# Joining two half-width products into one 512-column product, with the halves added on ScalarE and GpSimd

## The chip, the core and the metric

The kernel runs on one core of a Trainium2 chip. A core has five engines with queues of their own: TensorE (matrix products; "PE" in the profile, its weight loads "PEld"), VectorE ("DVE"), ScalarE ("ACT"), GpSimd ("POOL") and SyncE ("SP", which here only issues transfers). SBUF is the on-chip memory with 128 partitions; PSUM holds the results of products in banks of 128x512 float32. The metric is the device time of one execution in microseconds (us); lower is better.

## The reference

The program is a decoder trunk of two layers over a sequence of 512 positions with 1024 features, in float32. Each layer is a feed-forward block, a mixer (a causal convolution module beside differential attention), and a second feed-forward block:

```python
def swiglu(h, w_gate, w_up, w_down):
    return (jax.nn.silu(h @ w_gate) * (h @ w_up)) @ w_down

for l in range(DEPTH):
    x = x + 0.5 * swiglu(rms_norm(x, ffn1_norm[l]), ffn1_w_gate[l], ffn1_w_up[l], ffn1_w_down[l])
    h = rms_norm(x, mix_norm[l])
    a, g, q, k, v = jnp.split(h @ w_in[l], splits, axis=-1)
    ...
    x = x + jnp.concatenate([conv_out, diff_out], axis=-1) @ w_out[l]
    x = x + 0.5 * swiglu(rms_norm(x, ffn2_norm[l]), ffn2_w_gate[l], ffn2_w_up[l], ffn2_w_down[l])
```

The hidden width `D_FF` is 2816, that is 22 blocks of 128. The change touches the four feed-forward blocks only.

## The kernel before, in words

**Split operands.** Every float32 operand of a large product is held as two parts: a high part in a rounded type (`float32r`) and a low part, the rest. A product is then three products: high weight by high feature, high by low, low by high. The weights come from memory as `wraw` (128x512) and are split in `parts_of` (L101, L102): ScalarE copies into `whi`, VectorE subtracts `raw - hi` into `wlo`. Both operands of that subtraction lie in SBUF. In the mixer some of these subtractions are given to GpSimd instead.

**Seven products.** The 22 hidden blocks of a feed-forward block are done in three parts (`PARTS`): six in the plain way, and two times eight by a scheme in the manner of Strassen and Winograd, which makes two output blocks by two column halves (`HS` = 256 columns each) with seven half-size products instead of eight. For that, sums of weights are formed: `Sums` loads a base with SyncE (`wsum`, L162), adds a second block to it with an accumulating transfer of GpSimd's queue (L160), and two more sums are made on VectorE (L175, L176). Sums of features (`th`, `tl` for the inputs; `yh`, `yl` for the hidden values) are made on VectorE.

- `seven` does the gate and up projections of one hidden block, called a group below. It has 16 groups in a feed-forward block, 64 in the program. Its products are named by weight and feature: `u2u1`/`t1`, `u2`/`t4`, `g1`/`b11`, `g2`/`b21`, `all`/`b22`, `g1u2u1`/`t2`, and in `rest` `g1u1`/`t3`. Each is a loop over four contraction blocks with three products of 256 columns, L434. It uses two PSUM banks; `a`, `d` are the halves of the first and `b`, `c` of the second. ScalarE copies partial results into the SBUF tile `keep` (L439, L443, L448), VectorE combines them (L451, L456, L457, L460), and ScalarE applies the silu (L452).
- `rest` of a group is run as `before()` within the next group, between its second and third products (t4 and b11).
- `Hidden.add` makes the hidden values' parts (L483, L484) and their sums (L489 to L494).
- `Pair` does the same seven products for two output blocks of the down projection: `head`, `body` and `finish`, with products at L523. There are four pairs after each part of eight, 32 in the program; the first of each four (`m == 0`) has an order of its own, and the very last one ends in `finish_halves`.

**What sets the order.** A scheduler of the framework orders each engine's instructions from dependences and its own estimate; the first product of each loop is kept in program order (`keep_in_program_order`), and some splits are held behind named instructions (`behind`). Buffers are rings: 9 `whi`, 9 `wlo`, 5 `wraw`, 4 `wsum`, three pairs of PSUM banks, 2 `keep`. Each engine does its queue strictly in that order, so an instruction that waits holds those behind it.

Of the kernel before, what the change touches and what calls it, by code (L numbers as in the profile page):

```python
# [18 lines left out]
P = 128  # L19
# [51 lines left out]
def trunk(ctx: ExitStack, tc: tile.TileContext, xt, par, lamv, relb, onehot,  # L71
# [12 lines left out]
    def f32(ap):  # L84
        return ap.bitcast(F32)
# [120 lines left out]

    x = act.tile([P, KT, SEQ], F32, tag="x", name="x")

    acth = act.tile([P, KT, SEQ], F32R, tag="acth", name="acth")
    actl = act.tile([P, KT, SEQ], F32R, tag="actl", name="actl")  # L210
# [11 lines left out]
    S.activation(small.tile([P, 1], F32, tag="first", name="first", bufs=1), f32(ones_r[:, P : P + 1]), AF.Copy)  # L222
# [152 lines left out]
    class Halves:  # L375
# [4 lines left out]
        def __init__(self, fp, pr, r):  # L380
            self.th = fp.tile([P, 3, KT // 2, HS], F32R, tag="th", name="th")
            self.tl = fp.tile([P, 3, KT // 2, HS], F32R, tag="tl", name="tl")

            self.whole = []
            four = [fp.tile([P, 4, SEQ], F32, tag=tag, name="hn") for tag in ("yh", "yl")]
            free = [t[:, n] for t in four for n in range(4)]
# [27 lines left out]

    saves = []

    def seven(halves, w, banks, fp, before, last):
# [7 lines left out]
        g = keep[:, 0::2]  # L425
# [12 lines left out]
        go(c, "u2u1", "t1", first=True)  # L438
        S.activation(keep[:, 3], c, AF.Copy)  # L439
        go(d, "u2", "t4", first=True)  # L440
        before()
        go(a, "g1", "b11")
        S.activation(keep[:, :2], banks[0].rearrange("p (n c) -> p n c", n=2), AF.Copy)  # L443
        go(b, "g2", "b21")
        if not last:
            go(c, "all", "b22")
        go(a, "g1u2u1", "t2")
        saves.append(S.activation(keep[:, 2], a, AF.Copy))  # L448
        if last:
            go(c, "all", "b22")  # L450
# [3 lines left out]
        def rest(out=None):  # L454
            go(a, "g1u1", "t3")
# [9 lines left out]
    class Hidden:  # L465

        def __init__(self, fp, n):
            self.fp, self.n, self.parts = fp, n, [None] * (2 * n)
            self.th = fp.tile([P, 3, n, HS], F32R, tag="yh", name="yh")
            self.tl = fp.tile([P, 3, n, HS], F32R, tag="yl", name="yl")  # L470

        def add(self, mm, rest):
# [8 lines left out]
            hi = self.fp.tile([P, SEQ], F32R, tag=f"hh{mm}", name="hh")  # L481
            lo = self.fp.tile([P, SEQ], F32R, tag=f"hl{mm}", name="hl")
            self.big = S.activation(hi, h, AF.Copy)  # L483
            V.tensor_tensor(lo, h, f32(hi), op=ALU.subtract)  # L484
            self.parts[k] = hi, lo
# [11 lines left out]
        def get(self, name):  # L497
# [4 lines left out]
            return lambda j: tuple(t[:, c : c + HS] for t in self.parts[k0 + j])  # L502

    class Pair:

        def __init__(self, hid, fp, m, m2):
            self.hid, self.m, self.m2 = hid, m, m2
            self.kc, self.kd = (1, 3) if m == 0 else (3, 1)
# [681 lines left out]
```

## Time and profile before

| | |
|---|---|
| median of 3 runs | 1769.01 us (1768.8 to 1769.22) |
| the profiled execution | 1769.0 us, span 1767.2 us |
| TensorE busy | 1758.8 us |
| VectorE busy | 1472.1 us |
| ScalarE busy | 1037.1 us |
| GpSimd busy | 515.7 us |
| granted TensorE clock | 1.000 |

The span is the time from the first to the last instruction. Busy time is the time in which an engine has at least one instruction in work. Products overlap in TensorE's pipeline, so the mean duration of one (283 ns at L434) is longer than the spacing at which they follow each other. A row of the groups reads: line, engine, operation, output and inputs, shapes, count, then busy us and mean ns of one, then the engine's idle time just before them and what ended it. In the timeline a row begins with its start and its duration in us. In the table of stages a row gives, after the stretch and its length, the busy us of each engine and its instructions, then the granted clock, the share of the DMA engines and GB/s.

### The profile page before, as it was taken

What the parts mean: (1) busy time and instruction counts of PE and PEld (TensorE: products, weight loads), DVE (VectorE), ACT (ScalarE), POOL (GpSimd) and SP (SyncE); (2) the same over time, 40 slices, a digit from 0 to 9 for tenths busy, and PEclk for the clock granted to TensorE, in tenths of its full rate; (3) what the DMA queues carried; (4) which work ended last, traced back from release to release, by engine and by line L of the source; (5) the groups of instructions that cost most, each with busy time, mean ns of one, the idle gap of its engine ahead of it and who ended that gap; (6) DMA issues with size and microseconds to landing.
All of it is one profiled execution on the core that took longest, in us unless ns stands there. A gap on an engine that the chain in (4) does not pass through costs nothing.

```text
span 1767.2 us, 32964 instructions
## 1 busy us (share of the span) xinstructions
PE 1758.8 (100%) x11852; PEld 1621.2 (92%) x11852; DVE 1472.1 (83%) x2646; ACT 1037.1 (59%) x1955; POOL 515.7 (29%) x497
## 2 busy tenths in 40 slices
PE   9999999999999999999999999999999999999998
PEld 7799999988788899999988999999887888999998
DVE  7969888969877969989987798999698678698887
ACT  6546566755865436566644565666559554465664
POOL 1011112169970011212200121121798600112122
PEclk9999999999999999999999999999999999999999
DMA  7457777533223457677544576776231234576774
GB/s 229 129 138 185 172 188 190 138 120 100 68 78 114 126 129 178 171 198 179 141 143 111 147 177 172 198 166 166 91 114 49 96 102 139 134 183 163 201 183 127
DMA packets 166613, 257.78 MB, mean 146 GB/s; under 512 B 19271, under 2 KB 63318, under 8 KB 166448
## 3 DMA queue, kind: packets, MB, share of 16 engines
q1 hardware_dynamic: 129600, 201.25, 35.5%
q0 software_dynamic: 36416, 54.12, 18.7%
q8 instruction: 93, 1.52, 0.4%
q14 instruction: 72, 0.59, 0.1%
q10 hardware_dynamic: 432, 0.29, 0.1%
HBM read 253.48 MB, written 3.42 MB: 145 GB/s over the span
## 4 chain that ended last, share of the span: by engine, by line
PE 97%; DVE 1%; POOL 1%; ACT 1%; issue 0%; DVEq 0%; POOLq 0%
PE ps_pair L434 37%; PE ps_pair L523 18%; PE ps_pair L200 9%; PE ps_pair L203 9%; PE ps_pair L204 9%; PE ps_out L200 2%; PE ps_out L203 2%; PE ps_out L204 2%; PE ps_pair L842 2%; PE ps_pair L843 2%; PE ps_pair L841 2%; PE ps_sc L958 1%; PE ps_v L872 1%; PE ps_v L873 1%; PE ps_v L871 1%; POOL wlo L102 0%
## 5 line engine op out<-in xcount | busy, mean ns | idle before, releaser
L101 ACT ACTIVATE whi<-wraw 128x512 fp32r<-128x512 f32 x744 | 452.9, 627 | 397.4 <-PE ps_pair L203 166.3
L102 DVE TENSOR_TENSOR wlo<-wraw,whi 128x512 fp32r<-128x512 f32 x640 | 426.2, 685 | 111.5 <-ACT whi L101 104.2
L160 POOL DMA_DIRECT2D wsum<-in_gu x128 | 112.0, 904 | 700.4 <-DMA wsum<-in_gu 270.7
L434 PE MATMUL ps_pair<-acth,wlo 128*128 128x256 f32 x1024 | 289.8, 283 | 0.0
L434 PE MATMUL ps_pair<-actl,whi 128*128 128x256 f32 x1024 | 289.8, 283 | 0.0
L434 PE MATMUL ps_pair<-acth,whi 128*128 128x256 f32 x1024 | 289.8, 283 | 0.0
L434 PE MATMUL ps_pair<-th,whi 128*128 128x256 f32 x768 | 217.3, 283 | 0.0
L434 PE MATMUL ps_pair<-tl,whi 128*128 128x256 f32 x768 | 217.3, 283 | 0.0
L434 PE MATMUL ps_pair<-th,wlo 128*128 128x256 f32 x768 | 217.3, 283 | 0.0
L200 PE MATMUL ps_pair<-acth,whi 128*128 128x512 f32 x512 | 200.7, 394 | 0.3 <-DVE gs L653 0.3
L203 PE MATMUL ps_pair<-actl,whi 128*128 128x512 f32 x512 | 199.7, 390 | 0.0
L204 PE MATMUL ps_pair<-acth,wlo 128*128 128x512 f32 x512 | 199.3, 390 | 0.0
L434 PEld LDWEIGHTS ps_pair<-actl,whi 128*128 128x128 f32 x1024 | 196.6, 192 | 0.2
L434 PEld LDWEIGHTS ps_pair<-acth,whi 128*128 128x128 f32 x1024 | 196.6, 192 | 0.2
L434 PEld LDWEIGHTS ps_pair<-acth,wlo 128*128 128x128 f32 x1024 | 196.6, 192 | 0.0
L160 POOL DMA_DIRECT2D wsum<-in_dn x112 | 98.9, 1112 | 269.4 <-DMA wsum<-in_dn 55.7
L434 PEld LDWEIGHTS ps_pair<-th,whi 128*128 128x128 f32 x768 | 147.5, 192 | 0.0
L434 PEld LDWEIGHTS ps_pair<-tl,whi 128*128 128x128 f32 x768 | 147.5, 192 | 0.0
L434 PEld LDWEIGHTS ps_pair<-th,wlo 128*128 128x128 f32 x768 | 147.5, 192 | 0.0
L102 POOL TENSOR_TENSOR wlo<-wraw,whi 128x512 fp32r<-128x512 f32 x104 | 137.4, 1345 | 30.4 <-ACT whi L101 19.4
L523 PE MATMUL ps_pair<-hh,whi 128*128 128x256 f32 x512 | 144.9, 283 | 0.0
L523 PE MATMUL ps_pair<-hl,whi 128*128 128x256 f32 x512 | 144.9, 283 | 0.0
(209 smaller groups left out, 4446.5 us busy)
## 6 DMA issues: line engine op xcount, KB each, us to landing
wraw<-in_gu SPq DMA_DIRECT2D x280, 256.0 KB, 3.4
wsum<-in_gu SPq DMA_DIRECT2D x128, 256.0 KB, 3.7
wsum<-in_gu POOLq DMA_DIRECT2D x128, 256.0 KB, 4.7
wraw<-in_dn SPq DMA_DIRECT2D x68, 256.0 KB, 3.4
wraw<-in_wqkv SPq DMA_DIRECT2D x48, 256.0 KB, 2.7
wraw<-in_wout SPq DMA_DIRECT2D x48, 256.0 KB, 2.7
wraw<-in_dn SPq DMA_DIRECT2D x64, 128.0 KB, 4.0
wraw<-in_wag SPq DMA_DIRECT2D x32, 256.0 KB, 3.0
```

What stands on the lines that cost most here:

```text
L101: S.activation(hi, raw, AF.Copy)
L102: (eng or V).tensor_tensor(out=lo, in0=raw, in1=f32(hi), op=ALU.subtract)
L160: nc.gpsimd.dma_start(dst[:, to], src, accum_op=ALU.add)
L200: first = T.matmul(ps, wh, xh, start=start, stop=False)
L203: T.matmul(ps, wh, xl, start=False, stop=False)
L204: T.matmul(ps, wl, xh, start=False, stop=stop)
L434: mm = T.matmul(ps, l, r, start=first and i == j == 0, stop=False, skip_group_check=True)
L523: mm = T.matmul(ps, s[:, f], r, start=side not in self.begun, stop=False, skip_group_check=True)
L841: T.matmul(ps[n], xh[:, t], wh, start=k == 0, stop=False)
L842: T.matmul(ps[n], xh[:, t], wl, start=False, stop=False)
L843: T.matmul(ps[n], xl[:, t], wh, start=False, stop=k == KT - 1)
L871: T.matmul(ps, xh[:, t], wh, start=k == 0, stop=False)
```

## The change

In five of the seven products (t1, t4, b11, t2, t3) the two products through the large (high) weights become one of 512 columns: the feature's high part goes into one half of a PSUM bank and its low part into the other. The third product (low weight by high feature) stays at 256 columns and goes into the first half. g2/b21 and all/b22 stay as they were. For this, the high and low parts of the features must lie in one tile: `acth`, `actl` become the two halves of `acts`, `th`, `tl` of `ts`, `yh`, `yl` of `ys`, and `hh`, `hl` of `hs`.

Since a result now lies in two halves of a bank, the halves must be added. ScalarE copies both into SBUF (`keep`, and a new small tile `low`), and GpSimd adds them there, seven adds of 128x256 per group. In a down pair the same is done where `split` is set (`m > 0`, but not in the very last pair); the first pair of each four joins only t3. Some small tiles get shared names.

```diff
+    def both_columns(bank, w, both, pin, start=False):
+        (wh, wl), xh = w, both[:, 0]
+        mm = T.matmul(bank.rearrange("p (n c) -> p n c", n=2), wh, both, start=start, stop=False, skip_group_check=True)
+        if pin:
+            tc.keep_in_program_order(mm)
+        T.matmul(bank[:, :HS], wl, xh, start=False, stop=False, skip_group_check=True)
...
-        go(c, "u2u1", "t1", first=True)
-        S.activation(keep[:, 3], c, AF.Copy)
-        go(d, "u2", "t4", first=True)
+        wide(banks[1], "u2u1", "t1", first=True)
+        S.activation(keep[:, 2:], two, AF.Copy)
+        G.tensor_tensor(keep[:, 3], keep[:, 2], keep[:, 3], op=ALU.add)
+        wide(banks[0], "u2", "t4", first=True)
+        S.activation(keep[:, :2], pair, AF.Copy)
+        G.tensor_tensor(keep[:, 1], keep[:, 0], keep[:, 1], op=ALU.add)
         before()
-        go(a, "g1", "b11")
-        S.activation(keep[:, :2], banks[0].rearrange("p (n c) -> p n c", n=2), AF.Copy)
-        go(b, "g2", "b21")
+        wide(banks[0], "g1", "b11", first=True)
+        S.activation(g, pair, AF.Copy)
+        G.tensor_tensor(keep[:, 0], keep[:, 0], keep[:, 2], op=ALU.add)
+        go(b, "g2", "b21", first=True)
         if not last:
             go(c, "all", "b22")
-        go(a, "g1u2u1", "t2")
+        wide(banks[0], "g1u2u1", "t2")
+        low = fp.tile([P, HS], F32, tag="low", name="low", bufs=1)
+        S.activation(low, d, AF.Copy)
+        G.tensor_tensor(low, low, keep[:, 3], op=ALU.add)
         saves.append(S.activation(keep[:, 2], a, AF.Copy))
+        G.tensor_tensor(keep[:, 2], keep[:, 2], low, op=ALU.add)
...
         def rest(out=None):
-            go(a, "g1u1", "t3")
+            wide(banks[0], "g1u1", "t3")
+            low = fp.tile([P, HS], F32, tag="low", name="low", bufs=1)
+            S.activation(low, d, AF.Copy)
+            for n in (1, 3):
+                G.tensor_tensor(keep[:, n], keep[:, n], low, op=ALU.add)
             V.tensor_tensor(d, a, keep[:, 3], op=ALU.add)
             V.tensor_tensor(a, a, keep[:, 1], op=ALU.add)
...
+            self.split = m > 0 and not plain
...
+                if self.split:
+                    self.wide(self.banks[0], w["u2"], "t4", first=True)
+                    S.activation(self.keep[:, :2], both, AF.Copy)
+                    self.total(1, 0, 1)
+                    before()
+                    self.wide(self.banks[0], w["g1"], "b11", first=True)
+                    self.early = S.activation(self.keep[:, 0:3:2], both, AF.Copy)
+                    self.total(0, 0, 2)
+                    self.begun.discard(1)
+                    go(b, w["g2"], "b21")
+                    go(c, w["all"], "b22")
+                    self.wide(self.banks[0], w["g1u2u1"], "t2")
+                    low = self.low()
+                    G.tensor_tensor(low, low, self.keep[:, 3], op=ALU.add)
+                    saves.append(S.activation(self.keep[:, 2], a, AF.Copy))
+                    G.tensor_tensor(self.keep[:, 2], self.keep[:, 2], low, op=ALU.add)
```

The added lines that the order below names are, in the new numbering: L457, L460, L464, L471, L473 and L484, GpSimd's adds of a group (totals of t1, t4 and b11, two for t2, two for t3); L470, L472, L482, ScalarE's copies for t2 and t3. Of the old lines L451 is now L476, L456 and L457 are L485 and L486, L460 is L489, L483 and L484 are L512 and L513.

GpSimd's queue in the up groups of the first feed-forward block. Before, only the accumulating transfers stand there:

```order
L160 DMA wsum<-in_gu 128x512 [waits DMAHW6_49,DMASW3_49,DVE_49]
L160 DMA wsum<-in_gu 128x512 [waits DMASW4_49,DMAHW2_49,DVE_49,Activation_49]
L160 DMA wsum<-in_gu 128x512 [waits DMASW5_49,DMAHW3_49,DMASW1_49,DVE_49]
L160 DMA wsum<-in_gu 128x512 [waits DMASW6_49,DMAHW7_49,DVE_49,Activation_49]
L160 DMA wsum<-in_gu 128x512 [waits DMAHW0_49,DMASW7_49,DVE_49]
```

and now, for one group:

```order
L160 DMA wsum<-in_gu 128x512 [waits DMAHW4_49,DMASW0_49,DVE_49]
L473 TENSOR_TENSOR keep<-keep,low 128x256 [waits Activation_49,Pool_49]
L457 TENSOR_TENSOR keep<-keep 128x256 [waits Activation_49]
L160 DMA wsum<-in_gu 128x512 [waits DMAHW5_49,DMASW1_49,DVE_49]
L460 TENSOR_TENSOR keep<-keep 128x256 [waits Activation_49]
L484 TENSOR_TENSOR keep<-keep,low 128x256 [waits Activation_49]
L484 TENSOR_TENSOR keep<-keep,low 128x256
L464 TENSOR_TENSOR keep<-keep 128x256 [waits Activation_49]
L471 TENSOR_TENSOR low<-low,keep 128x256 [waits Activation_49]
```

Seven adds stand between and around two accumulating transfers; each transfer also waits for its base load (DMAHW).

VectorE's queue around the end of a group, before:

```order
L451 TENSOR_TENSOR ps_pair<-ps_pair,keep 128x512 [waits Activation_49]
L494 TENSOR_TENSOR yl<-ht,yh 128x3x256 [waits Activation_49]
L102 TENSOR_TENSOR wlo<-wsum,whi 128x512 [waits DMASW4_49,PE_49,Activation_49]
L102 TENSOR_TENSOR wlo<-wraw,whi 128x512 [waits DMAHW6_49,PE_49,Activation_49]
L102 TENSOR_TENSOR wlo<-wraw,whi 128x512 [waits DMAHW7_49,PE_49,Activation_49]
L456 TENSOR_TENSOR ps_pair<-ps_pair,keep 128x256 [waits PE_49]
L102 TENSOR_TENSOR wlo<-wraw,whi 128x512 [waits DMAHW0_49,Activation_49]
```

and now:

```order
L476 TENSOR_TENSOR ps_pair<-ps_pair,keep 128x512 [waits Pool_49]
L523 TENSOR_TENSOR ys<-ht,ys 128x3x256 [waits Activation_49]
L102 TENSOR_TENSOR wlo<-wraw,whi 128x512 [waits DMAHW7_49,PE_49,Activation_49]
L102 TENSOR_TENSOR wlo<-wraw,whi 128x512 [waits DMAHW0_49,PE_49,Activation_49]
L175 TENSOR_TENSOR wraw<-wsum,wraw 128x512
L485 TENSOR_TENSOR ps_pair<-ps_pair,keep 128x256 [waits Activation_49,Pool_49]
L176 TENSOR_TENSOR wraw<-wraw 128x512 [waits DVE_49]
```

The two combinations wait for GpSimd where they waited for ScalarE and for TensorE, and the one after t3 (L456, now L485) stands one weight split and one sum later.

113 lines of the change are left out of this document (76 added, 37 removed).

## The prediction

> **What bounds the kernel now.** I read the page's busy shares and the chain that ended last, then the chain in order of time, then a table of the four stages of the first feed-forward block, then the groups of VectorE in one stage.
>
> ```profile
> PE 1758.8 (100%) x11852; PEld 1621.2 (92%) x11852; DVE 1472.1 (83%) x2646; ACT 1037.1 (59%) x1955; POOL 515.7 (29%) x497
> PE 97%; DVE 1%; POOL 1%; ACT 1%; issue 0%; DVEq 0%; POOLq 0%
> 107.34 80.63 PE ps_pair L434 x672
> 71.82 0.39 PE L200 MATMUL ps_pair<-acth,whi 128*128 128x512 f32 x1
> ...
> 73.86 0.39 PE L200 MATMUL ps_pair<-acth,whi 128*128 128x512 f32 x1
> ```
>
> TensorE carries 97% of the chain. The mean of one 256-column product in the groups is no price, since products overlap; the spacing is. In the chain 672 products of 256 columns take 80.63 us, 120.0 ns each. In the timeline, nine steps of 512-column products run from 71.82 to 73.86, 226.7 ns each. Two narrow products cost 240.0 ns, one wide one 226.7: joining a pair saves 13.3 ns.
>
> ```profile
> core 0: us, PE busy (x) PEld busy (x) DVE busy (x) ACT busy (x) POOL busy (x), PEclk, DMA share, GB/s
> 107.00:188.00 81.00, 81.00 (x676) 80.96 (x675) 69.51 (x121) 50.40 (x94) 14.71 (x17) 1.00 0.70 176
> 188.00:227.00 39.00, 39.00 (x327) 39.00 (x327) 34.57 (x59) 21.36 (x43) 6.91 (x8) 1.00 0.69 167
> 231.00:309.00 78.00, 78.00 (x652) 78.00 (x651) 69.54 (x124) 48.75 (x91) 17.48 (x20) 1.00 0.76 188
> 309.00:348.00 39.00, 39.00 (x326) 38.96 (x325) 37.39 (x65) 27.65 (x54) 8.83 (x10) 1.00 0.53 130
> sum 237.00, PE 237.00 PEld 236.92 DVE 211.00 ACT 148.16 POOL 47.93; mean PE 59.25 PEld 59.23 DVE 52.75 ACT 37.04 POOL 11.98
> ```
>
> These are the stages that the change touches (up products, down products, twice); there are four such blocks. TensorE is full, but VectorE is next: 211.0 of 237 us, and 37.39 of 39 in the last stage. Its slack is 26 us a block, 104 us in all. What adds more than that to VectorE takes the bound from TensorE.
>
> ```profile
> L451 DVE TENSOR_TENSOR ps_pair<-ps_pair,keep 128x512 f32<-128x512 f32 x8 | 5.6, 694 | 2.6 <-PE ps_pair L434 2.1 <-ACT keep L448 0.6
> L460 DVE SCALAR_TENSOR_TENSOR hid<-ps_pair,keep 128x512 f32<-128x512 f32 x7 | 4.8, 684 | 0.0
> L456 DVE TENSOR_TENSOR ps_pair<-ps_pair,keep 128x256 f32<-128x256 f32 x7 | 3.0, 429 | 0.9 <-PE ps_pair L434 0.8
> L457 DVE TENSOR_TENSOR ps_pair<-ps_pair,keep 128x256 f32<-128x256 f32 x7 | 3.0, 427 | 0.1
> L102 DVE TENSOR_TENSOR wlo<-wraw,whi 128x512 fp32r<-128x512 f32 x38 | 25.4, 686 | 6.9 <-ACT whi L101 6.4
> ```
>
> Of the 69.5 us in the first stage only the first four groups (16.4 us, 24%) take one operand from PSUM. The other 76%, the weight splits of the last row above all, read two SBUF tensors.
>
> **TensorE's part.** In five of seven products, weight-high times feature-high and feature-low become one product. The order lists count 11,703 products before and 9,931 after: 1,772 fewer. 1,772 x 13.3 ns = 23.6 us, all on TensorE's queue and so on the path, if nothing else ends last: 1769.0 - 23.6 = 1745.4. [...]
>
> **ScalarE's part.** Per group of seven up products it copies 512 instead of 256 columns after t1, and adds one 512-column copy (t4) and two 256-column ones.
>
> ```profile
> L443 ACT ACTIVATE keep<-ps_pair 128x512 f32<-128x512 f32 x8 | 4.8, 598 | 7.4 <-PE ps_pair L434 7.4
> L439 ACT ACTIVATE keep<-ps_pair 128x256 f32<-128x256 f32 x8 | 3.0, 370 | 0.0
> ```
>
> (0.598 - 0.370) + 0.598 + 2 x 0.370 = 1.57 us a group, 12.5 on the 50.4 of 81 us in that stage. It stays below VectorE: nothing on the path. What covers the added wait of TensorE on the t4 copy (g1's wide product restarts the same bank) is the previous group's t3, four steps of 226.7 + 120.0 ns = 1.39 us, against a matmul's tail of some 0.3 and a copy of 0.598. If a split (0.63) stands in front of the copy, the cover is short by some 0.2; over 64 + 23 places between 0 and 87 x 0.63 = 55 us. I take 0, since TensorE is not what ends last below; the end counts where it is.
>
> **GpSimd's part.** Added are 617 adds of 128x256 with both operands in SBUF: 7 for each of 64 up groups, 7 for each of 23 split pairs, 8 single ones. None of that size is in the trace.
>
> ```profile
> L913 POOL TENSOR_TENSOR yp<-yp,prod 128x512 f32<-128x512 f32 x78 | 101.2, 1298 | 7.2 <-ACT prod L912 4.5
> L1000 POOL TENSOR_TENSOR so<-so,se 128x4 f32<-128x4 f32 x8 | 1.6, 201 | 7.3 <-DVE so L999 7.3
> ```
>
> Halfway between, 201 + (1298 - 201)/2 = 0.75 us (ends 0.20 and 1.30). Seven are 5.3 us on GpSimd in a group of 10 us, beside two accumulating transfers of 0.9: it fits. But does VectorE keep its pace beside them? In the feed-forward stages of before GpSimd only issues transfers, so nothing there answers. One place in the mixer does; VectorE first, GpSimd below:
>
> ```profile
> 503.88 0.68 DVE L941 SCALAR_TENSOR_TENSOR u<-th,u 128x512 f32<-128x512 f32 x1
> 504.87 0.69 DVE L1003 TENSOR_TENSOR ov<-ps_o,rs_y 128x512 f32<-128x512 f32 x1
> ...
> 506.58 1.77 DVE L941 SCALAR_TENSOR_TENSOR u<-th,u 128x512 f32<-128x512 f32 x1
> ...
> 509.97 1.78 DVE L941 SCALAR_TENSOR_TENSOR u<-th,u 128x512 f32<-128x512 f32 x1
> ```
> ```profile
> 503.25 1.59 POOL L260 TENSOR_TENSOR rs_y<-so,mhalf 128x4 f32<-128x4 f32 x1
> 504.80 9.81 POOL L102 TENSOR_TENSOR wlo<-wraw,whi 128x512 fp32r<-128x512 f32 x6
> ```
>
> L941 reads two SBUF tensors: 0.68 us beside a tiny GpSimd instruction, 1.77 and 1.78 beside a stream of 128x512 subtractions on GpSimd. L1003, with one operand in PSUM, keeps its 0.69 beside the same stream. GpSimd loses too: six in 9.81 us are 1.64 each, not 1.30. So the two do not read two SBUF tensors side by side; one stands until the other is done. The Trainium skill ("SBUF — State Buffer", "Who interferes with whom") says the same as a rule, for a VectorE instruction with two SBUF inputs against a GpSimd one that reads SBUF, and it names tensor_tensor, the form of L102, of which no row here shows the meeting.
>
> The price of an add: the 128x512 instruction puts L941 back by 1.77 - 0.68 = 1.09; an add of half the length by 1.09 - 0.55 = 0.54, where 0.55 is half of 1298 - 201. VectorE pays it when the add comes while it is busy with two SBUF operands (0.76) and the next instruction is again one (0.76); if the next has a PSUM operand (0.24), some 0.1 is left over; if the add comes during a PSUM instruction (0.24), a rest of some 0.33. That is 0.76 x (0.76 x 0.54 + 0.24 x 0.1) + 0.24 x 0.33 = 0.41 us an add, 617 x 0.41 = 253 us.
>
> **VectorE's waits and the queues.** L485 (formerly L456) and L476 (L451) now wait for GpSimd, with splits queued behind them: after t3 come a copy of 0.37 and two adds, 1.9 us. While VectorE stands there, those adds block nothing, so waits replace part of the blocking; I add 0, with an upper end of 3% idle (1.2 of 39 us in the fullest stage): 34 us. GpSimd's accumulating transfers now stand between the adds and can be late by one or two, 0.75 to 1.5 us.
>
> ```profile
> 140.56 0.87 POOL L160 DMA_DIRECT2D wsum<-in_gu  x1 [1.22 <-DVE wlo L102]
> wsum<-in_gu POOLq DMA_DIRECT2D x128, 256.0 KB, 4.7
> 146.53 0.62 ACT L101 ACTIVATE whi<-wsum 128x512 fp32r<-128x512 f32 x1
> ```
>
> Issued at 140.56 and landed 4.7 later, 145.3, the sum is read at 146.53: 1.3 us of cover, which a longer group widens. I take 0. SyncE's order is the same but for four rows near the end; VectorE's and TensorE's own instruction counts on other lines do not move, the re-tagged small tiles cost nothing.
>
> **Sum.** VectorE needs 4 x 211 + 253 us where the four blocks had 4 x 237: 253 - 104 = 149 us more, and TensorE's 23.6 us vanish in its waiting. Against the profiled execution (1769.0, span 1767.2; the median of the runs is 1769.01, the same): 1769 + 149 = 1918.
>
> **Rivals.**
> - *Gain.* Splits of the form TENSOR_TENSOR are not held up, or the adds fall into VectorE's gaps. Then TensorE stays the bound: 1745, up to 1769 if part of the 55 us for the t4 copy comes. It decides how much an add costs VectorE: with 154 adds and 26 us of slack a block, over 26/154 = 0.17 us is a loss, and under (26 - 6)/154 = 0.13, 6 being TensorE's saving, the gain is whole. For it: no row shows L102 held up. Against: same operands, same engine pair as L941, and a 76% chance to meet.
> - *Near-perfect packing.* GpSimd's adds run just when VectorE has PSUM operands (24% of its time, 51 us a block), at 0.2 to 0.26 us an add: 617 x 0.23 = 142, less 104: +38, so 1785 to 1830. Against it: what releases the adds is ScalarE, not VectorE.
> - *Worse: GpSimd's queue.* An accumulating transfer that waits for its base load holds the adds behind it; ScalarE's copy after g1 waits for them, TensorE for that copy. Half a microsecond to two a group on top: 1918 + 64 x 1 = 1982, to 2046.
>
> **How the numbers follow.** Forecast (port shared, 1830 to 1985) 0.62; packing 0.13; queue (above 1985) 0.12; gain 0.13, of which 0.11 is faster and 0.02 within 0.2% (3.5 us, about what a measurement of this kernel tells from no change). The time is the forecast's, 1918. The range leaves out the gain and the top third of the queue's case: 1780 to 2030. Faster 0.11, same 0.02, slower 0.87.
>
> **What would show it.** In the profile of the changed kernel: spacing 226.7 and 120.0 for the new pair (step 1); L102 on VectorE well above 686 ns, near 0.9 to 1.0 on average, in the feed-forward stages and unchanged in the mixer; GpSimd's adds near 0.75 or longer; VectorE's busy share above 90% and TensorE no longer 97% of the chain there, waiting for wlo. If L102 stays at 686 ns the forecast is wrong and the gain is right; if L102 is lengthened but the stages grow little, the packing; if ScalarE's copies wait for GpSimd and GpSimd for transfers, the queue.

## The result, and the profile after

The changed kernel takes 2095.05 us (median of 4 runs, 2085.34 to 2096.3) against 1768.9: 1.1832 times as long, 95% interval 1.1815 to 1.1849. Predicted were 1918, at most 2030. The direction was right, the size was not: 326 us more instead of 149.

The page of the changed kernel, busy shares and chain:

```profile
span 2092.5 us, 30666 instructions
PE 1847.5 (88%) x10080; PEld 1585.5 (76%) x10080; DVE 1763.8 (84%) x2646; ACT 1140.6 (55%) x2224; POOL 1073.7 (51%) x1114
PE 61%; DVE 21%; issue 6%; ACT 6%; POOL 4%; DMA 2%; DVEq 0%; SPq 0%; ACTq 0%; POOLq 0%
```

VectorE executes 2,646 instructions, as before, and is busy 1763.8 - 1472.1 = 291.7 us longer. TensorE's share of the chain falls from 97% to 61%, but no other engine takes over: the busiest of them, VectorE, is at 84%. The four stages of the first feed-forward block, as a table of windows (81, 39, 78 and 39 us long before the change):

```profile
core 0: us, PE busy (x) PEld busy (x) DVE busy (x) ACT busy (x) POOL busy (x), PEclk, DMA share, GB/s
111.00:220.00 109.00, 91.06 (x539) 80.40 (x539) 97.88 (x126) 59.30 (x119) 64.22 (x72) 0.92 0.54 129
220.00:265.00 45.00, 40.97 (x243) 36.67 (x244) 37.25 (x55) 24.81 (x51) 24.22 (x27) 0.92 0.64 155
265.00:370.00 105.00, 79.18 (x472) 68.69 (x470) 99.19 (x122) 56.61 (x114) 63.96 (x73) 0.95 0.59 135
370.00:420.00 50.00, 43.18 (x252) 38.61 (x252) 40.44 (x62) 28.48 (x58) 27.63 (x29) 0.89 0.41 101
sum 309.00, PE 254.40 PEld 224.37 DVE 274.76 ACT 169.20 POOL 180.04; mean PE 63.60 PEld 56.09 DVE 68.69 ACT 42.30 POOL 45.01
```

VectorE stands still for 309.0 - 274.8 = 34 us of these stretches; before it was 26 of 237. The idle time from which the prediction paid 104 us was not used up, it grew. TensorE now has gaps, and a granted clock of 0.89 to 0.95 that was 1.00. What it waits for, in the table of waits (engine, tile and line that wait, then what they wait for: total us, times, longest):

```profile
PE ps_pair L209 <- ACT keep L459: 90.6, 47, 4.4
PE ps_pair L209 <- ACT keep L463: 55.2, 15, 6.2
PE ps_pair L209 <- ACT keep L472: 35.4, 28, 2.4
PE ps_pair L209 <- ACT keep L602: 30.1, 19, 3.4
```

These are ScalarE's copies of the banks after t4, g1 and t2, and the one after t4 in the down pairs. In the groups by form, VectorE's weight splits with two SBUF operands are lengthened (686 ns before), its operations on PSUM are not:

```profile
L102 DVE TENSOR_TENSOR wlo<-wraw,whi 128x512 fp32r<-128x512 f32 x640 | 569.0, 908 | 90.9 <-ACT whi L101 89.9
L102 DVE TENSOR_TENSOR wlo<-wsum,whi 128x512 fp32r<-128x512 f32 x192 | 167.6, 880 | 26.4 <-ACT whi L101 26.2
...
L476 DVE TENSOR_TENSOR ps_pair<-ps_pair,keep 128x512 f32<-128x512 f32 x64 | 44.2, 690 | 40.2 <-POOL keep L473 30.3 <-PE ps_pair L446 9.8
L489 DVE SCALAR_TENSOR_TENSOR hid<-ps_pair,keep 128x512 f32<-128x512 f32 x64 | 44.0, 687 | 2.6
```

Where the time goes is seen in the timeline, VectorE first, GpSimd below:

```profile
158.42 0.68 DVE L102 TENSOR_TENSOR wlo<-wsum,whi 128x512 fp32r<-128x512 f32 x1
159.02 2.73 DVE L102 TENSOR_TENSOR wlo<-wraw,whi 128x512 fp32r<-128x512 f32 x1
161.67 3.20 DVE L513 TENSOR_TENSOR hs<-hid,hs 128x512 fp32r<-128x512 f32 x1
164.79 0.69 DVE L476 TENSOR_TENSOR ps_pair<-ps_pair,keep 128x512 f32<-128x512 f32 x1
```
```profile
159.47 1.03 POOL L473 TENSOR_TENSOR keep<-keep,low 128x256 f32<-128x256 f32 x1
160.16 1.03 POOL L457 TENSOR_TENSOR keep<-keep 128x256 f32<-128x256 f32 x1
161.27 0.88 POOL L160 DMA_DIRECT2D wsum<-in_gu  x1
161.88 1.05 POOL L460 TENSOR_TENSOR keep<-keep 128x256 f32<-128x256 f32 x1
162.57 1.73 POOL L484 TENSOR_TENSOR keep<-keep,low 128x256 f32<-128x256 f32 x2
```

The split that began at 159.02 ends at 161.75, 0.56 us after the second of two adds that start 0.69 apart; the next instruction stands through three adds. VectorE does not get in between adds that follow each other like this.

How such a hold-up reaches TensorE is seen right behind it, on ScalarE first and then on TensorE (in brackets the idle time before, and what ended it):

```profile
165.51 0.60 ACT L477 ACTIVATE keep<-ps_pair 128x512 f32<-128x512 f32 x1 [4.55 <-DVE ps_pair L476]
166.00 0.59 ACT L463 ACTIVATE keep<-ps_pair 128x512 f32<-128x512 f32 x1
```
```profile
166.65 0.50 PE L209 MATMUL ps_pair<-ts,whi 128*128 128x512 f32 x1 [1.87 <-ACT keep L463]
```

The combination L476 stands in VectorE's queue behind the held-up L513. ScalarE's silu (L477) waits 4.55 us for it, the copy after g1 (L463) stands behind the silu in ScalarE's queue, and TensorE waits 1.87 us for that copy. The two rows of the waits table for this way:

```profile
ACT whi L101 <- DVE wraw L176: 208.0, 76, 5.8
ACT keep L477 <- DVE ps_pair L476: 76.1, 53, 5.0
```

The first was 69.9 us before the change, the same wait for the combination 10.7. All of ScalarE's waits for VectorE add up to 385 us, against 117 before.

### The profile page after: what moved, and what is told of

Same layout as the page of the kernel before. It is cut to its first block, busy times and chain, and to the rows that moved or that the text cites. A ratio compares the mean times of both kernels' runs of the same rounds, so it can differ in the third digit from the quotient of the medians.

```text
span 2092.5 us, 30666 instructions
## 1 busy us (share of the span) xinstructions
PE 1847.5 (88%) x10080; PEld 1585.5 (76%) x10080; DVE 1763.8 (84%) x2646; ACT 1140.6 (55%) x2224; POOL 1073.7 (51%) x1114
## 4 chain that ended last, share of the span: by engine, by line
PE 61%; DVE 21%; issue 6%; ACT 6%; POOL 4%; DMA 2%; DVEq 0%; SPq 0%; ACTq 0%; POOLq 0%
PE ps_pair L209 11%; DVE wlo L102 8%; PE ps_pair L200 8%; PE ps_pair L204 8%; PE ps_pair L203 8%; PE ps_pair L212 5%; PE ps_pair L446 5%; PE ps_pair L559 3%; ACT whi L101 3%; DVE wraw L175 2%; PE ps_out L200 1%; DVE wraw L176 1%; PE ps_out L203 1%; PE ps_out L204 1%; PE ps_pair L922 1%
## 5 line engine op out<-in xcount | busy, mean ns | idle before, releaser
L102 DVE TENSOR_TENSOR wlo<-wraw,whi 128x512 fp32r<-128x512 f32 x640 | 569.0, 908 | 90.9 <-ACT whi L101 89.9
L209 PE MATMUL ps_pair<-ts,whi 128*128 128x512 f32 x768 | 294.7, 418 | 90.6 <-ACT keep L463 55.2
L209 PE MATMUL ps_pair<-acts,whi 128*128 128x512 f32 x512 | 207.2, 435 | 90.6 <-ACT keep L459 90.6
L209 PEld LDWEIGHTS ps_pair<-ts,whi 128*128 128x128 f32 x768 | 150.1, 195 | 135.9 <-ACT keep L463 58.8
L212 PE MATMUL ps_pair<-ts,wlo 128*128 128x256 f32 x768 | 221.5, 288 | 0.0
L446 PE MATMUL ps_pair<-acts,whi 128*128 128x256 f32 x1024 | 203.0, 299 | 0.0
L209 PEld LDWEIGHTS ps_pair<-acts,whi 128*128 128x128 f32 x512 | 103.8, 203 | 129.9 <-ACT keep L459 106.6
L200 PE MATMUL ps_pair<-acts,whi 128*128 128x512 f32 x512 | 200.3, 395 | 0.2 <-DVE gs L732 0.2
L204 PE MATMUL ps_pair<-acts,wlo 128*128 128x512 f32 x512 | 199.9, 391 | 0.0
L203 PE MATMUL ps_pair<-acts,whi 128*128 128x512 f32 x512 | 199.7, 390 | 0.0
L102 DVE TENSOR_TENSOR wlo<-wsum,whi 128x512 fp32r<-128x512 f32 x192 | 167.6, 880 | 26.4 <-ACT whi L101 26.2
L446 PEld LDWEIGHTS ps_pair<-acts,whi 128*128 128x128 f32 x1024 | 174.8, 210 | 4.4
L212 PE MATMUL ps_pair<-acts,wlo 128*128 128x256 f32 x512 | 151.8, 297 | 0.0
L446 PE MATMUL ps_pair<-acts,wlo 128*128 128x256 f32 x512 | 151.7, 296 | 0.0
L212 PEld LDWEIGHTS ps_pair<-ts,wlo 128*128 128x128 f32 x768 | 151.5, 197 | 0.0
L102 POOL TENSOR_TENSOR wlo<-wraw,whi 128x512 fp32r<-128x512 f32 x104 | 137.3, 1343 | 25.6 <-ACT whi L101 18.6
L471 POOL TENSOR_TENSOR low<-low,keep 128x256 f32<-128x256 f32 x64 | 64.4, 1007 | 154.5 <-ACT low L470 154.5
L484 POOL TENSOR_TENSOR keep<-keep,low 128x256 f32<-128x256 f32 x128 | 131.2, 1180 | 8.7 <-ACT low L482 8.6
```

The costliest lines, as they stand in the source:

```text
L102: (eng or V).tensor_tensor(out=lo, in0=raw, in1=f32(hi), op=ALU.subtract)
L200: first = T.matmul(ps, wh, xh, start=start, stop=False)
L203: T.matmul(ps, wh, xl, start=False, stop=False)
L204: T.matmul(ps, wl, xh, start=False, stop=stop)
L209: mm = T.matmul(bank.rearrange("p (n c) -> p n c", n=2), wh, both, start=start, stop=False, skip_group_check=True)
L212: T.matmul(bank[:, :HS], wl, xh, start=False, stop=False, skip_group_check=True)
```

## The experiments

Medians stand against the kernel before on the same chip (1768.56 to 1769.16); brackets hold the ratio's 95% interval. Where an expectation or the prediction says 617 adds, 609 are adds that these runs change; the other eight are subtractions of the first pairs, and they stay in every variant of the changed kernel.

### The change without its adds

`wide_only`: joined products, copies of the same halves as before, no adds.

```diff
-        S.activation(keep[:, 2:], two, AF.Copy)
-        G.tensor_tensor(keep[:, 3], keep[:, 2], keep[:, 3], op=ALU.add)
+        S.activation(keep[:, 3], c, AF.Copy)
...
-        S.activation(keep[:, :2], pair, AF.Copy)
-        G.tensor_tensor(keep[:, 1], keep[:, 0], keep[:, 1], op=ALU.add)
```

> The changed kernel with the 512-column products, but ScalarE copies only the halves that it copied before, and nothing is added: the feature-low halves of five products are left out of the output. What is left of the change is TensorE's part alone. By the spacings of the trace of before (226.7 ns for a joined pair, 240.0 for two narrow products) 1,772 joins save 23.6 us: 1745. If TensorE's gain had been the mis-sized term (saving 2.5 ns a pair) the time is 1765; if joined products hurt in themselves (both parts of the features lie in one tile now, with other due times), it is above 1769. L102 on VectorE stays at 686 ns in either case.

Measured: 1756.82 [0.9915, 0.9945]. A gain of 12.3 us, 7.0 ns a join (12.3/1,772): about half of the 13.3, more than the 2.5 that the expectation gives as the other case. The timeline of TensorE shows why:

```profile
139.63 0.40 PE L209 MATMUL ps_pair<-acts,whi 128*128 128x512 f32 x1
139.87 0.28 PE L212 MATMUL ps_pair<-acts,wlo 128*128 128x256 f32 x1
139.99 0.40 PE L209 MATMUL ps_pair<-acts,whi 128*128 128x512 f32 x1
140.23 0.28 PE L212 MATMUL ps_pair<-acts,wlo 128*128 128x256 f32 x1
...
141.05 0.40 PE L446 MATMUL ps_pair<-acts,whi 128*128 128x256 f32 x2
```

Four such pairs of steps, one of 512 columns and one of 256, take 141.05 - 139.63 = 1.42 us, 0.355 each. Less 0.120 for the narrow step, the wide one takes 0.235, not the 0.227 of the unbroken stream that the prediction used.

`no_adds`: the changed kernel with ScalarE's copies, each GpSimd add left out.

```diff
-        G.tensor_tensor(keep[:, 3], keep[:, 2], keep[:, 3], op=ALU.add)
...
-                G.tensor_tensor(keep[:, n], keep[:, n], low, op=ALU.add)
```

> The changed kernel with all added copies of ScalarE, but without GpSimd's 617 adds (the feature-low halves are copied and then left out of the output; eight subtractions of the first pairs stay). Theory A, the adds are the cause (they stop VectorE, and TensorE's waits for ScalarE's copies follow from late VectorE work ahead of the copies): TensorE's waits for keep disappear almost wholly, VectorE's L102 is back at 686 ns, and the time is 1745 to 1760. Theory B, the copies are the cause (TensorE restarts a bank that ScalarE is still copying, whatever GpSimd does): the 211 us of TensorE's waits for keep and low in the changed kernel stay, with the lower clock behind them, and the time is 1950 or more. In between, 1760 to 1800, the 0 to 55 us that the prediction named for the wait on the t4 copy.

Measured: 1807.00 [1.0197, 1.0227]. The copies cost 50.2 us over `wide_only`, near the 55 that the prediction kept as the end, not the 0 that it took. L102 is back at 695 ns. TensorE's waits there are for the copies after t4, in the groups and in the down pairs:

```profile
PE ps_pair L209 <- ACT keep L463: 19.6, 32, 1.8
PE ps_pair L209 <- ACT keep L606: 14.9, 17, 1.6
```

The adds then cost 2095 - 1807 = 288 us, and the change is -12 + 50 + 288 = 326. Each term is the price of one part on top of those before it, in this order.

### What an add does to VectorE

`memset_adds` and `two_memsets`: `G.memset(to, 0.5)` for each add, once or twice.

> The changed kernel with each of GpSimd's 617 adds replaced by a memset of the same 128x256 destination: all semaphores, waits and queue places stay, GpSimd writes as much, but reads no SBUF (the halves are not added, so the sums are left out of the output; the eight subtractions stay). Theory A (two instructions that each read two SBUF tensors exclude each other): L102 stays near 686 ns, the time is that of the kernel without adds, 1745 to 1775. Rival C, it is GpSimd's place in the chain (ScalarE to GpSimd to VectorE, accumulating transfers behind the adds) and not the reads: the waits stay, 1900 or more with L102 at 686 ns. Rival D, any GpSimd work on SBUF stops VectorE: L102 is lengthened wherever it meets a memset, and the time scales with the memset's duration.

> As the run with a memset for each add, but with two memsets for each, so that GpSimd's step in the chain (ScalarE's copy, GpSimd, VectorE or ScalarE) is some 0.8 to 1.0 us long, like an add of the changed kernel (1.0 to 1.3 us); the sums are left out of the output. Rival C, the length of GpSimd's step keeps the others waiting: between a third and all of the 288 us that the adds cost over the kernel without them, 1900 or more. Theory A, the reads do it: TensorE and VectorE hardly notice, 1800 to 1820.

Measured: 1801.17 [1.0164, 1.0194] and 1807.22 [1.0204, 1.0238], as without adds (1807.00). L102 with two memsets:

```profile
L102 DVE TENSOR_TENSOR wlo<-wraw,whi 128x512 fp32r<-128x512 f32 x640 | 432.4, 691 | 112.2 <-ACT whi L101 104.7 <-PE ps_pair L209 6.5
```

Neither GpSimd's writing nor another step of some 0.9 us in the chain costs anything; the rivals C (GpSimd's place in the chain) and D (any GpSimd work) fall. One flaw: a memset reads nothing, so ScalarE need not wait to overwrite an operand, and not all waits stayed as the expectation said. That comes back below.

`one_input`: `G.tensor_scalar(to, p, 0.0, None, op0=ALU.add)`, one SBUF operand.

> The changed kernel with each of GpSimd's 617 adds of two SBUF tensors replaced by a copy-like operation with one SBUF input (its first operand plus zero; the other half is left out of the output). Theory A in the narrow form (both engines must read two SBUF tensors): VectorE is not held up, L102 near 690 ns, 1800 to 1820. Theory A in the wide form (any read of SBUF by GpSimd stops a two-input VectorE instruction): L102 is lengthened, and by the durations of the trace of before (128x512 with one input 0.79 us, with two 1.30) some 0.6 of the 288 us come: about 1980.

Measured: 1910.69 [1.0784, 1.0820], and L102 is lengthened:

```profile
L102 DVE TENSOR_TENSOR wlo<-wraw,whi 128x512 fp32r<-128x512 f32 x640 | 466.6, 746 | 114.4 <-ACT whi L101 113.3
...
L175 DVE TENSOR_TENSOR wraw<-wsum,wraw 128x512 f32<-128x512 f32 x96 | 81.0, 844 | 0.0
```

So the wide form: one read operand on GpSimd is enough. The Trainium skill ("SBUF — State Buffer", "Who interferes with whom") says that a two-input VectorE instruction contends with a GpSimd one that reads SBUF and not with one that only writes; the 1911 us here and the 1807 us of the memsets agree. The cost was 104 us over no adds, less than the 173 expected. It is not all VectorE's: VectorE's busy time grows by 74 us, and ScalarE waits 115 us in sum to overwrite what these operations (1.49 us each on `keep`) still read.

`adds_on_vector`: `V.tensor_tensor(to, p, q, op=ALU.add)`, whole product computed.

> The changed kernel with the 617 adds on VectorE instead of GpSimd; the whole product is computed. VectorE pays each add in full: half of a 128x512 one of 0.686 us with a fixed part, an estimate of 0.35 to 0.43 us, 216 to 265 us; less the 104 us of slack and with TensorE's 23.6 us lost in its waiting: 1880 to 1930. If VectorE's load alone had set the time of the changed kernel, the two are near each other at equal cost per add (0.47 us there, measured as VectorE's growth of 292 us). If the long stalls (VectorE standing behind a whole row of adds, up to 5.5 us, and TensorE's clock falling behind them) made the difference between 1918 and 2095, this kernel has few TensorE clock losses and comes out well below 2000.

Measured: 1878.56 [1.0596, 1.0632], just below the low end. In the windows of its first block VectorE is nearly full:

```profile
sum 271.00, PE 251.15 PEld 222.50 DVE 262.81 ACT 176.89 POOL 48.62; mean PE 62.79 PEld 55.62 DVE 65.70 ACT 44.22 POOL 12.15
```

It grows by 1660.1 - 1480.0 = 180 us over `no_adds` (0.30 an add), and the time by 72: here VectorE's idle time does cover the rest. On GpSimd the same adds lengthen VectorE's busy time by 284 us and the time by 288. The excess is 216 us, of which 104 is VectorE's busy time; the other 112 is VectorE's idle time, which covers 108 us in one kernel and nothing in the other.

### Rows, sums that are waited for, the clock

`gapped_adds`: a wait between adds. For each add there now stand two instructions, both also held in program order:

```diff
-        G.tensor_tensor(to, p, q, op=ALU.add)
+        tc.keep_in_program_order(G.tensor_tensor(to, p, q, op=ALU.add))
+        tc.keep_in_program_order(G.tensor_copy(mark, to[:, :1]))
```

> The changed kernel, whole product computed, with a one-column copy on GpSimd behind each of the 617 adds; the copy reads the sum, so GpSimd must finish each add before it begins the next. In the trace of the changed kernel adds that do not depend on each other start 0.69 us apart while each lasts 1.03, and VectorE stands until the last of them is done (2.73 and 3.20 us for instructions of 0.68). In the run of seven chained adds they start 1.03 apart and VectorE gets one instruction in after each. Theory T, the rows without a gap make the excess over the adds on VectorE (2095 against 1879): the longest L102 falls from 4.75 to below 2 us and the time to 1900 to 1990, although GpSimd has 617 instructions more. Rival G, GpSimd's adds cost what they cost by their number and length: 2095 or, with the copies' time on top, 2100 to 2200.

Measured: 2051.18 [1.1578, 1.1613]. 44 us less although GpSimd has 609 instructions more; VectorE's busy time falls by 62.6 us to 1701.2. Rows without a gap are a part, far from all; theory T (the rows make the excess) was too large by 60 us and more. The gain is net: ScalarE's waits for GpSimd to let go of `keep` and `low` grow from 73 to 166 us.

`unread_rows` and `unread_chained`: the adds write to a spare tile, in turn to its two halves or always to one.

```diff
-        G.tensor_tensor(to, p, q, op=ALU.add)
+        G.tensor_tensor(spare[0][:, len(turn) % 2], p, q, op=ALU.add)
```

> The changed kernel with the same 617 adds of the same operands on GpSimd at the same places, but written in turn to two halves of a spare tile that nobody reads, so that neither VectorE nor ScalarE waits for a sum (the sums are left out of the output). Theory H, the hold-up of VectorE by the reads is the whole cause: within 40 us of the changed kernel, 2055 to 2095. Theory S, the waits for sums that are late because the adds themselves are held up make up the rest: the price found with 448 adds alone (0.267 us each net) times 617 is 165, on top of 1807 with the copies: 1970, plus up to 44 for rows without a gap: 1970 to 2015.

> As the run with unread sums, but all written to one half of the spare tile, so that each add waits for the one before it and VectorE gets in between. Theory S: about 1970 by the same sum, 1940 to 1985. Theory H: 2010 to 2050, as far below the changed kernel as the run with a copy behind each add (2051). The distance to the run with unread sums in rows is the price of the missing gaps alone: 15 us in the runs with 448 adds in a row, 44 in the changed kernel.

Measured: 2086.48 [1.1779, 1.1818] and 2034.73 [1.1492, 1.1534]. That nobody waits for a sum takes 9 us away from the changed kernel and 16 from `gapped_adds`; theory S, which put the waits for sums at 80 us and more, falls. These figures are net too: in `unread_rows` VectorE is busy 47 us longer than in the changed kernel (1810.7), and ScalarE waits 152 us instead of 73 to overwrite operands. The missing gap is worth 52 here.

`clock_kept`: six products of ones ahead of g1.

```diff
         before()
+        fill(6)
         wide(banks[0], "g1", "b11", first=True)
```

> The changed kernel with six 512-column products of ones into an unused bank on TensorE ahead of g1 in each of 64 up groups (1.36 us each, 87 us in all), where TensorE waits 90.6 us in sum for the copy after t4. The granted clock was 0.959 on the changed kernel, and steps of 0.43 and 0.21 us (half rate) behind long gaps cost some 74 us. Theory K, that lost clock is on the path: the half-rate steps go, and the time falls by 30 to 74 us, 2020 to 2065. Rival, the pace is VectorE's and GpSimd's, and TensorE's half rate lies inside its waiting: the clock rises and the time stays at 2080 to 2110, or grows where the products stand in the way, to 2180.

Measured: 2102.72 [1.1871, 1.1906], at a granted clock of 0.973 instead of 0.959: 8 us longer. No gain came from this rise of the clock. It does not settle the matter: half-rate steps were not gone altogether, and the added products make TensorE busy 64 us longer, of which a part can stand in the way and hide a gain.

### What the cover covers

The kernel before, with unread adds on GpSimd behind ScalarE's copies.

```diff
         S.activation(keep[:, 3], c, AF.Copy)
+        extra(keep[:, 3], 1)
...
+        extra(keep[:, 1], 2)
...
         saves.append(S.activation(keep[:, 2], a, AF.Copy))
+        extra(keep[:, 2], 2)
...
+            extra(keep[:, 3], 2)
```

> The kernel before (no joined product, no added copy) with 448 adds of 128x256 on GpSimd that read ScalarE's copies and write a spare tile which nobody reads: seven for each up group, released two and two by the copies. Theory A1, the price is what VectorE is held up (0.41 to 0.47 us an add): 184 to 211 us, less the 80 us of slack of the up stages (11.5 + 8.5 us a block): 1873 to 1900. Theory A2, VectorE's stalls themselves keep TensorE waiting and lower its clock, with or without a consumer of the sums: over 1930. Theory E, the excess comes from the waits for the sums and for the added copies: at or below 1880, with no lower granted clock.

The five others differ from this by their calls: `extra(keep[:, 2], 7)` behind t2 (in a row); the same with two targets in turn, of 16 bits each (no chain); one call each behind t1, g1 and t3 (three); `extra(keep[:, 3], 7)` behind t1; and for the other half

```diff
-        extra(keep[:, 2], 7)
+        G.tensor_copy(spare[:, :1], keep[:, 2, :1])
+        extra(keep[:, 1], 7)
```

> As the run with the adds alone, but all seven adds of an up group are released by one copy (that of t2) and stand in a row on GpSimd. If each add costs VectorE its own price wherever it stands, the time is that of the adds alone within 15 us. If VectorE, once it meets a row of adds, waits until the row ends, it stands up to seven times 0.69 = 4.8 us in each of 64 groups, some 4.4 us after the first instruction that still gets through: 282 less 80 us of slack, about 1970, with L102 instances above 4 us.

> As the run of seven adds in a row (1942), with the same adds at the same place, but writing in turn to two spare tiles (of 16 bits, for room), so that no add waits for the one before it. Theory T: they start 0.69 apart instead of 1.03, VectorE stands through whole rows (L102 of 3 to 5 us), and the time is above 1942: 64 rows of which VectorE loses most, 7 x 0.69 = 4.8 us, less 80 us of slack, gives up to 2000. Rival G, a shorter row occupies GpSimd for less time, and the time falls below 1942, to 1900 or so.

> The kernel before with only three of the seven unread adds in each up group (behind the copies of t1, g1 and t3), 192 in all. By the 448 adds alone (0.278 us of VectorE each) VectorE's busy time grows by 53 us, below the 80 us of its idle time in the up stages. Slack theory (the prediction's step: load against load): the idle time covers it, 1769 to 1780. No-cover theory (a hold-up comes where TensorE or ScalarE waits next, and is paid however much idle time stands elsewhere): 0.267 x 192 = 51, 1810 to 1825.

> As the run of seven chained adds in a row behind the copy of t2 (1942), with the row behind the copy of t1 instead, at the start of the group, away from VectorE's three PSUM operations that give back the banks. If the place in the group decides what a hold-up costs, the time moves by more than 20 us, down to the 1889 of the spread adds or below; if every hold-up of VectorE is paid alike, it stays at 1925 to 1960.

> As the run of seven chained unread adds in a row behind the copy of t2 (1942), at the same place (a one-column copy of keep[2] releases the row), but the adds read keep[1] instead of keep[2]. ScalarE's silu overwrites keep[0] and keep[2] and not keep[1], so that it need not wait for the end of the row. Theory W: what makes the row behind t2 dear is not VectorE's hold-up at that place but ScalarE, which waits to overwrite what GpSimd still reads (107 us of such waits with the adds alone, 92 in the row, none behind t1's copy and none with three adds): those waits go, and the time falls to that of the row behind t1's copy, 1845 to 1875. Place theory: VectorE is held up just as much behind t2, and the time stays at 1920 to 1945.

Measured, with VectorE's growth from the pages and ScalarE's waits on GpSimd for `keep` from the tables of waits:

| run | adds a group, where, what they read | time | VectorE busy, more | ScalarE waits | time, more |
|---|---|---|---|---|---|
| three_adds | 3, t1, g1, t3; halves 3, 1 | 1774.28 [1.0018, 1.0042] | 57.9 | 0 | 5.7 |
| row_at_t1 | 7 behind t1; half 3 | 1853.34 [1.0464, 1.0506] | 146.6 | 0 | 84.8 |
| row_other_half | 7 behind t2; half 1 | 1889.90 [1.0671, 1.0709] | 138.3 | 42.8 | 121.0 |
| adds_alone | 7 spread; halves 3, 1, 2 | 1888.62 [1.0658, 1.0690] | 124.6 | 107.3 | 120.0 |
| adds_in_a_row | 7 behind t2; half 2 | 1941.94 [1.0960, 1.0993] | 142.6 | 91.8 | 173.3 |
| row_no_chain | the same, no chain | 1956.52 [1.1039, 1.1076] | 168.7 | 54.2 | 187.6 |

```profile
ACT keep L461 <- POOL spare L420: 91.8, 38, 5.7
```
```profile
ACT keep L462 <- POOL spare L457: 36.3, 12, 6.0
```

The first row is of the adds in a row, the second of the same row reading the other half. With three adds ScalarE never waits for an add, and the idle time covers nine tenths of VectorE's growth. Behind t1's copy ScalarE waits for no add either, and yet the idle time covers only 62 of 147 us. The tables of waits of that run show the way of the other 85 us that the changed kernel's timeline showed above, through ScalarE's waits for VectorE:

```profile
ACT whi L101 <- DVE wraw L176: 193.8, 63, 5.2
PE ps_pair L440 <- ACT keep L456: 37.1, 30, 3.2
```

All of ScalarE's waits for VectorE are 348 us there, 222 with three adds, 117 before; with three adds TensorE waits for no copy into `keep`. So ScalarE can stand for some time at no price, but not for long. No run takes this way away by itself.

Behind t2's copy the idle time covers none. There the adds read `keep[2]`, which ScalarE's silu overwrites; it stands in ScalarE's queue ahead of the copies for which TensorE waits. Reading `keep[1]` at the same place takes 49 us of those waits away and 52 us of the time: theory W (ScalarE waits to overwrite what GpSimd still reads) explains more than half of the 89 us between the two rows behind t2 and t1. The 37 us that stay go with the 43 us of waits that stay (36 of them for the releasing copy, which queues behind the previous row) or with the place; that is not separated. The adds alone do not fit one line either: more waits than in the row, but 53 us less time. Their 1889 lies in A1's bracket by two errors that cancel: 0.28 us an add instead of 0.41 to 0.47, and 5 us of cover instead of 80.

That VectorE waits for the end of a row falls for chained adds: it gets one instruction in per add (VectorE, then GpSimd, of the adds in a row). Without the chain its longest split grows from 1.84 to 2.95 us, and the time by 15, the way T had it, though less far. The rows are of the chained run:

```profile
133.10 0.42 DVE L466 TENSOR_TENSOR ps_pair<-ps_pair,keep 128x256 f32<-128x256 f32 x1
133.43 0.76 DVE L102 TENSOR_TENSOR wlo<-wraw,whi 128x512 fp32r<-128x512 f32 x1
134.12 1.10 DVE L175 TENSOR_TENSOR wraw<-wsum,wraw 128x512 f32<-128x512 f32 x1
```
```profile
130.68 5.01 POOL L420 TENSOR_TENSOR spare<-keep 128x256 f32<-128x256 f32 x5
```

### Half of the adds on VectorE

`late_on_vector` and `early_on_vector`: the changed kernel with the adds behind t2 and t3, or those behind t1, t4 and g1, as `V.tensor_tensor`.

> The changed kernel, whole product computed, with the four adds behind the copies of t2 and t3 on VectorE (348 in all) and the three behind t1, t4 and g1 left on GpSimd (261). Place theory (a hold-up behind t2 and t3 meets the instructions that give the banks back): nearly all of the 216 us between the adds on GpSimd (2095) and on VectorE (1879) go, 1860 to 1900. Number theory (each add on GpSimd carries the same share of the 216 us): 261/617 of it stays, about 1970.

> The reverse: the three adds behind t1, t4 and g1 on VectorE (261), the four behind t2 and t3 on GpSimd (348). Place theory: most of the excess stays, 2040 to 2100. Number theory: 348/617 of 216 us stays on top of 1879, about 2001.

Measured: 2006.14 [1.1300, 1.1381] and 2011.20 [1.1345, 1.1383]. The place theory falls for the changed kernel: both halves cost alike. The three early adds a group that are left on GpSimd cost 128 us over all on VectorE, the four late ones 133. The theory that goes by number comes near in the second run (2001) and is 36 us short in the first (1970). The late run shows a way (group and wait of that run):

```profile
L460 POOL TENSOR_TENSOR keep<-keep 128x256 f32<-128x256 f32 x64 | 124.3, 1942 | 2.6 <-ACT keep L459 2.6
```
```profile
ACT keep L463 <- POOL keep L460: 126.2, 36, 4.8
```

VectorE, which now has 348 adds of its own with two SBUF operands, holds up GpSimd: L460 takes 1.94 us on average (1.27 in the changed kernel). ScalarE's copy after g1 overwrites `keep[0]` and `keep[2]`, which the adds behind t1 and t4 read, and waits 126 us for them; TensorE waits for that copy. In the changed kernel the same wait shows 26 us, with 24 and 20 us at two more copies. Taking it away there was not tried. In the early run ScalarE waits only 25 us in all for GpSimd, and the price is the same, so this wait cannot be the only way.

No version that computes the whole product beats the kernel before: the 20 joins of a group save 20 x 7.0 ns = 0.14 us, and a single one of its seven adds costs VectorE 0.30.

## Why the prediction was right and wrong

The step that failed is the cover of 104 us (item 4). Against the forecast's 149 us stand 288 for the adds, 50 for the copies and -12 for the joins. Of the 177 us that the forecast lacks, 104 are the cover, 35 the adds and 50 the copies, less the 12 that the joins gave.

1. *Joins (23.6 us).* Sign right, size half: 12.3. The spacing 226.7 came from an unbroken stream of 512-column products; between narrow ones the step takes 235 ns. So the sign "226.7 for the new pair" did not come.
2. *ScalarE's copies ("I take 0").* For the case that TensorE ends last the prediction kept 55, and `no_adds`, where it does (81% of the chain), shows 50. The 0 rested on VectorE ending last instead. That is not how the changed kernel looks: TensorE has 61% of the chain, VectorE 21%, and TensorE waits for ScalarE's copies. What the copies cost beside the adds is not measured by itself.
3. *The price of an add (0.41 us, 253).* The mechanism is confirmed by memsets, one input and the lengthened L102. VectorE's growth was 284 us over 609 adds, 0.47 each, 31 us more than the sum. The sum lacked that two and more adds without a gap are one hold-up; with gaps put in, 63 us of VectorE's time went, so this alone is large enough for the 31. GpSimd's add was put at 0.75 and took 0.9 to 1.3 on average, held up itself.
4. *The cover (104 us), the step that failed.* Load was set against load, as if any idle time could pay for any hold-up. Of 284 us none was covered, and VectorE's idle time grew. Three adds a group were covered, own instructions of VectorE were covered (108 of 180), rows behind t2 were not. What happened in place of cover: a hold-up makes ScalarE stand, ScalarE's copies for TensorE queue behind that, and TensorE waits (224 us in sum for `keep` and `low`, 35 without the adds). Two ways lead there. ScalarE waits to overwrite what GpSimd still reads: 52 us in a pair of runs that differ in what the adds read, and 73 us of waits in the changed kernel. And ScalarE waits for VectorE's late results: 385 us of waits there against 114 without the adds, followed in the timeline and by the row behind t1, but not taken away by a run. The prediction's third rival named the first way ("ScalarE's copy after g1 waits for them, TensorE for that copy"), but expected late transfers as its cause and stopped at 2046. How the 288 us divide between the two ways in the changed kernel stays open.
5. *VectorE's waits for sums (0, end 34).* Within its end: 9 to 16 us net. The end itself took 1.2 us of idle time in 39; the fullest stage has 39.00 - 37.39 = 1.6, which would make it some 45.
6. *Late transfers (0).* No sign of a large cost: memsets on the same queue were free, and GpSimd's waits for the base loads add up to 326 us before and after.

Of the signs named ahead, L102 (0.9) and TensorE's share of the chain came as said. VectorE above 90% came in one stage of the four (81 to 94%), and TensorE waits for ScalarE's copies, not for wlo. The gain and the packing fall: the price an add was 0.47, over their 0.17 and 0.26.

## What to carry to other kernels

Idle time of an engine is no account from which any delay can be paid. Ask of each new delay which in-order queue it stands in and who waits at its end; here a sum of loads held for three adds a group and failed for seven. And when work moves to GpSimd, count three things beside its length: VectorE's two-operand instructions that stand meanwhile, who waits for their results, and who must wait before overwriting GpSimd's operands.

## What the hardware showed beside that

- Adds on GpSimd that did not depend on each other started 0.69 us apart and let no two-operand VectorE instruction through (the rows from 159 to 164 us above); chained ones started 1.02 apart (5.01 us for five) and let one through each. The longest L102 was 5.1 us in the changed kernel and 1.84 in the chained row (both from the trace).
- The hold-up works both ways: in the run with the late adds on VectorE, GpSimd's add L460 took 0.71 us at its shortest (755.41, beside VectorE's L486, which reads PSUM), 1.94 on average, and 3.96 at 172.53, beside seven of VectorE's instructions that run there without a stop, two of them its adds L484.
- TensorE ran at half rate behind pauses: after waits of 2.12 and 1.75 us that end at 144.02 and 147.50 us of the changed kernel it steps 0.43 and 0.21 us, instead of 0.235 and 0.120, from 147.50 on, until 152:

```profile
149.58 0.63 PE L209 MATMUL ps_pair<-acts,whi 128*128 128x512 f32 x1
150.01 0.42 PE L212 MATMUL ps_pair<-acts,wlo 128*128 128x256 f32 x1
150.22 0.63 PE L446 MATMUL ps_pair<-acts,whi 128*128 128x256 f32 x2
...
152.14 0.48 PE L446 MATMUL ps_pair<-acts,whi 128*128 128x256 f32 x2
152.47 0.28 PE L446 MATMUL ps_pair<-acts,wlo 128*128 128x256 f32 x1
```
